# Differential attention scores on one Trainium2 core: six passes on 64 rows in place of four stacked passes on 128 rows

## The chip, the cores and the metric

The kernel runs on 1 core of one Trainium2 chip. The metric is the device time of one execution in microseconds (us). Engines are called as the profile calls them: PE is TensorE's matrix multiply, PEld its weight load, DVE is VectorE, ACT is ScalarE, POOL is GpSimd, SP is SyncE, which issues most DMAs. One measured execution of the kernel before was profiled; its instructions and waits are the trace that is read here.

## The reference, cut to what matters

The program is one step of a decoder layer: RWKV-7 time mixing and differential attention run as two branches on the same normalised input, are merged by gates, and an MLP follows. Float32 throughout. There are 512 prompt tokens and 8 samples of 8 tokens. The change touches the attention over the prompt. Each of the 4 heads has two parts, c = 0 and 1, of 64 channels; each part has its own scores and softmax, and the second softmax is subtracted from the first with a weight:

```python
def diff_attend(q, q_pos, segs, lam, slopes):
    ...
        s = jnp.einsum('bqhcd,bkhcd->bhcqk', q, k).astype(jnp.float32) * scale
        dist = q_pos[:, None] - k_pos[None, :]
        bias = -slopes[:, None, None] * dist.astype(jnp.float32)
        scores.append(jnp.where(dist >= 0, s + bias[None, :, None], NEG))
    p = jax.nn.softmax(jnp.concatenate(scores, axis=-1), axis=-1)
    attn = p[:, :, 0] - lam * p[:, :, 1]
    ...
```

The prompt is attended in blocks of 128 queries, with causal masking, so query block qb needs the first 128(qb+1) keys.

## The kernel before, in words

**Halves.** Products of float32 numbers are made from numbers in a shorter format (`F32R`). Each operand x is split: hi is x copied by ACT to `F32R`, lo is x - hi, made by DVE. A product is then three matmul passes that add up in one bank of PSUM: hi·hi, hi·lo and lo·hi. All dense projections are done so (`stream`, line 154): 8 pieces of 128 input channels, three passes each, 288 columns.

**Stages.** The input is normalised and the projections q, k and v of head 0 are made. Then, for each head h, `qkv(h)` (line 352) makes that head's projections, channels on the 128 rows and tokens along the columns, and `stacks(h)` (line 528) and four calls of `prompt(h, qb)` (line 542) do its attention over the prompt. Part 0 of a head lies in rows 0 to 63 of `qT` and `kT`, part 1 in rows 64 to 127. For heads 0 to 2 this overlaps with the projections of the next head. Beside head 3's blocks run the samples' attention (`sample`, line 622) and the first projections of the RWKV branch. The RWKV branch, the gates, the output projections and the MLP follow.

**The scores before.** `stacks` lays out, for each part cc, three operands of 128 rows by 512 columns. `qs` holds q's hi in the part's own 64 rows and q's lo in the other 64. `ks` holds k's hi in both. `kl` holds k's lo in the part's own rows, and zeros, set once at the start by POOL, in the others. One pass `qs`·`ks` over 128 rows is then hi·hi + lo·hi, and `qs`·`kl` is hi·lo: two passes a part, four a block (lines 548 and 549). For a head that takes six ACT operations and four DVE operations on 64 rows by 512 columns.

**After the scores.** `stt` on DVE scales each part's scores and adds the bias on the way from PSUM to the tile `sc`; DVE takes the maximum, ACT the exponential, DVE joins the two parts, PE transposes the result (`pt`) and multiplies it by v (`po`).

**Banks.** The scores of part cc go into the bank `cbank(cc)` (line 107), of which there is one for each part. The samples' scores use the same two banks, even samples the first and odd ones the second.

**What sets the order.** The kernel is written with priorities. Instructions of attention have the priority of their place in the program; dense passes have a later one (`FILL`), so that they fill in where nothing else is ready, and the evictions and splittings that feed them an earlier one (`FEED`). A scheduler orders each engine's instructions ahead of time, by priority among those that it reckons to be ready, and each engine then works through its list in order. `feed` (line 506) keeps several blocks under way, each at another of its steps, and `fill` (line 224) places a number of dense passes behind what was just issued.

Of the kernel before, what the change touches and what calls it, by code (L numbers as in the profile page):

```python
# [8 lines left out]
F32 = mybir.dt.float32  # L9
F32R = mybir.dt.float32r  # L10
# [5 lines left out]
P = 128  # L16
D = 1024
KT = D // P
NPR = 512
# [22 lines left out]
def tile_hybrid_step(ctx, tc, xT, xsT, ktab, vtab, s0T, ptab, w_in, vecs, w2a2, g2, lamv,  # L42
# [3 lines left out]
    PE, VE, AE, GE = nc.tensor, nc.vector, nc.scalar, nc.gpsimd  # L46
    PS = bass.MemoryType.PSUM

    def pool(name, bufs=1, stack=ctx, **kw):
        return stack.enter_context(tc.tile_pool(name=name, bufs=bufs, **kw))  # L50

    def f32(ap):
        return ap.bitcast(F32)
# [3 lines left out]
    def act(out, in_, func=AF.Copy, **kw):  # L57
        ring["act"] = AE.activation(out=out, in_=in_, func=func, **kw)  # L58

    def tt(out, a, b, op, eng=None):  # L60
        ins = (eng or VE).tensor_tensor(out=out, in0=a, in1=b, op=op)  # L61
        if eng is None:
            ring["tt"] = ins

    def stt(out, a, s, b, op0, op1):
        VE.scalar_tensor_tensor(out=out, in0=a, scalar=s, in1=b, op0=op0, op1=op1)

    def ts(out, a, s1, op0, s2=None, op1=ALU.bypass, eng=None):
        (eng or VE).tensor_scalar(out=out, in0=a, scalar1=s1, scalar2=s2, op0=op0, op1=op1)

    def mm(out, lhsT, rhs, start=True, stop=True):
        ring["mm"] = PE.matmul(out=out, lhsT=lhsT, rhs=rhs, start=start, stop=stop)  # L72
        return ring["mm"]

    def tr(out, in_, idn):
        ring["mm"] = PE.transpose(out=out, in_=in_, identity=idn)
# [14 lines left out]
    MUL, ADD, SUB, MAX = ALU.mult, ALU.add, ALU.subtract, ALU.max  # L91
# [9 lines left out]
    def bank(name):  # L101
        return psw.tile([P, 512], F32, tag="w", name=name)
# [4 lines left out]
    def cbank(i, name):  # L107
        return (psy if i else psc).tile([P, 512], F32, tag=f"c{i}", name=name)
# [131 lines left out]
    def rpow(dst, src, scale, eps):  # L240

        ts(dst, src, scale, MUL, eps, ADD)
        GE.tensor_tensor(out=dst, in0=dst, in1=mhalf[:dst.shape[0], :dst.shape[1]], op=ALU.pow)
# [27 lines left out]
    with tc.tile_pool(name="xin", bufs=2, reuse_waits="tile") as xin:  # L271
# [6 lines left out]
        for k in range(0, KT, 4):  # L278
            for j in range(3):
                with prio(FEED + 1000 + 10 * k + j):  # L280
                    name = f"raw_{'qkv'[j]}0_{k}"
                    if k == 0:
                        raw = ring["pool"].tile([P, 4, P], F32, tag="raw", name=name, bufs=3)
                    else:
                        raw = zw.tile([P, 1 + NX], F32, tag="z" if j else "tz", name=name,
                                      bufs=2 if j else 1)[:, :4 * P].rearrange("p (k w) -> p k w", k=4)
# [46 lines left out]
    ap = pool("ap", stack=attn, reuse_waits="tile")  # L333
    qT = ap.tile([P, HB, NT], F32, name="qT")
    kT = ap.tile([P, HB, NT], F32, name="kT")
# [75 lines left out]
    bp = ap.tile([P, HB, 512], F32, name="bp")  # L411
# [108 lines left out]
        for u in done:  # L520
            flight.remove(u)


    kl = ap.tile([P, 2, NPR], F32R, name="kl")
    for cc in range(2):
        GE.memset(kl[64 - 64 * cc:128 - 64 * cc, cc].bitcast(F32), 0.0)

    def stacks(h):

        qs = ap.tile([P, 2, NPR], F32R, tag="qs", name=f"qs{h}", bufs=1)  # L530
        ks = ap.tile([P, 2, NPR], F32R, tag="ks", name=f"ks{h}", bufs=1)
        for cc in range(2):
            own, oth = slice(64 * cc, 64 * cc + 64), slice(64 - 64 * cc, 128 - 64 * cc)
            q, k = qT[own, h, :NPR], kT[own, h, :NPR]
            act(qs[own, cc], q)
            tt(qs[oth, cc], q, f32(qs[own, cc]), SUB)
            act(ks[own, cc], k)
            act(ks[oth, cc], k)
            tt(kl[own, cc], k, f32(ks[own, cc]), SUB)
        return qs, ks  # L540

    def prompt(h, qb, ot, ss, qs, ks):
        L = P * (qb + 1)
        sc = ap.tile([P, 2, 512], F32, tag="sc", name=f"sc{h}{qb}", bufs=3)
        for cc in range(2):
            pss = cbank(cc, f"pss{h}{qb}{cc}")
            t = slice(qb * P, (qb + 1) * P)
            mm(pss[:, :L], qs[:, cc, t], ks[:, cc, :L], stop=False)
            mm(pss[:, :L], qs[:, cc, t], kl[:, cc, :L], start=False)
            stt(sc[:, cc, :L], pss[:, :L], 0.125, bp[:, h, 512 - L:], MUL, ADD)  # L550
        nmx = stat.tile([P, 2], F32, tag="nmx", name=f"nmx{h}{qb}", bufs=4)
        VE.tensor_reduce(out=nmx, in_=sc[:, :, :L], axis=AX.X, op=MAX, negate=True)
        z = stat.tile([P, 2], F32, tag="z", name=f"z{h}{qb}", bufs=4)
        for cc in range(2):
            act(sc[:, cc, :L], sc[:, cc, :L], AF.Exp, bias=nmx[:, cc:cc + 1],
                accum_out=z[:, cc:cc + 1])
        rz = stat.tile([P, 2], F32, tag="rz", name=f"rz{h}{qb}", bufs=4)
        VE.reciprocal(out=rz, in_=z)
        stt(rz[:, 1:2], rz[:, 1:2], nlam, z[:, 0:1], MUL, MUL)
        stt(sc[:, 0, :L], sc[:, 1, :L], rz[:, 1:2], sc[:, 0, :L], MUL, ADD)  # L560
        yield 1
        pt = bank(f"pt{h}{qb}")
        for kb in range(qb + 1):
            tr(pt[:, kb * P:(kb + 1) * P], sc[:, 0, kb * P:(kb + 1) * P], ident)
        attnT = ap.tile([P, 512], F32, tag="attnT", name=f"attnT{h}{qb}", bufs=3)
        act(attnT[:, :L], pt[:, :L])
        yield 1
        po = bank(f"po{h}{qb}")
        for kb in range(qb + 1):
            mm(po[:, :P], attnT[:, kb * P:(kb + 1) * P], vtok[:, kb, h],  # L570
               start=(kb == 0), stop=(kb == qb))
        ts(ot[:, qb], po[:, :P], rz[:, 0:1], MUL)
        junk = ap.tile([P, P], F32, tag="junk", name=f"junk{h}{qb}", bufs=1)
        act(junk, ot[:, qb], AF.Square, accum_out=ss[:, qb:qb + 1])
        if qb < 3:
            return
        rr = stat.tile([P, 4], F32, tag="rr", name=f"rr{h}")
        rpow(rr, ss, 1.0 / P, 1e-5)
        for qb in range(4):
            ts(ot[:, qb], ot[:, qb], rr[:, qb:qb + 1], MUL)  # L580
        yield 1
        yield 1
        pt = bank(f"pto{h}")
        for qb in range(4):
            tr(pt[:, qb * P:(qb + 1) * P], ot[:, qb], ident)
        obh = ap.tile([P, 512], F32, tag="obh", name=f"obh{h}", bufs=2)
        act(obh, pt, scale=subg)
        nc.gpsimd.dma_start(out=ob_d[h, :, :NPR], in_=obh)
# [76 lines left out]
    for h in range(HB):  # L665
        if h:
            qkv(h)
        for cc in range(2):
            GE.tensor_copy(
                out=qbd[64 * cc:64 * cc + 64, :, h, 8 * cc:8 * cc + 8],  # L670
                in_=qT[64 * cc:64 * cc + 64, h, NPR:].rearrange("p (b q) -> p b q", b=NB))
        ot = ap.tile([P, 4, P], F32, tag="ot", name=f"ot{h}", bufs=2)
        ss = stat.tile([P, 4], F32, tag="ss", name=f"ss{h}")
        qk = stacks(h)
        if h < HB - 1:
            for qb in range(4):
                feed(prompt(h, qb, ot, ss, *qk))
    waiting += [shifted(12), shifted(13)] + zs(0)
    for n in range(4):
        for unit in (prompt(HB - 1, n, ot, ss, *qk), sample(2 * n), sample(2 * n + 1)):  # L680
            feed(unit)
            fill(18)
# [12 lines left out]
    pss = bank("psq")  # L695
# [428 lines left out]
    for i, d in enumerate((0, 4, 1, 5, 2, 6, 3, 7)):  # L1124
# [4 lines left out]
        k = d % 4  # L1129
# [44 lines left out]
    qs = {}  # L1174
# [125 lines left out]
    rows = []  # L1300
    for d, n in enumerate((None, "t1", "b11", "t2", "b21", "t3", "b22", "t4")):
        if n:
            t = fp.tile([P, 2, 4, 288], F32R, tag=f"h_{n}", name=f"w3_{d}", bufs=1)
            t = t.rearrange("p i k t -> p (i k t)")
# [5 lines left out]
    for t0, n in LAST:  # L1310
# [47 lines left out]
        for d in range(KT):  # L1358
# [4 lines left out]
            if d + 1 in ends:  # L1363
                i = ends.index(d + 1)
# [119 lines left out]
```

## Time and profile before

| | |
|---|---|
| median of 3 runs | 1004.05 us (1003.92 to 1005.98) |
| the profiled execution, its own time | 1006.88 us |
| its span, first to last instruction | 1005.1 us |
| mean granted clock of TensorE | 0.993 of full |
| HBM read and written | 89.38 MB and 14.78 MB |
| DMA queue that loads most: share of 16 engines' span | 30.4% |
| score passes (tile `pss`) | 64, first start 39.3 us, last 151.6 us |

In the rows below a time comes first, then how long the instruction took, its engine, the line of the helper that recorded it, the operation, the tile that it writes and the tiles that it reads, the piece of TensorE's array (rows*columns), the shape, and the count. Most matmuls are recorded by one helper on line 72, so they are told apart by their tiles: `pss` is a block's scores, `ps_q`, `ps_k`, `ps_v` and `ps_z` are dense projections, `psb` and `pos` the samples' attention. Matmuls are pipelined: one lasts longer than the time to the start of the next, so what it costs is read from start to start. An idle time in brackets names the instruction that ended it.

### The profile page before, as it was taken

The numbers are of one execution on the slowest core, as the hardware profiler recorded it, in microseconds if no ns is written. First come the engines' busy times: TensorE is split into PE (matmuls) and PEld (weight loads), VectorE is DVE, ScalarE is ACT, GpSimd is POOL, SyncE is SP. The second block draws the span as 40 slices with busy tenths as digits, with TensorE's granted clock in tenths as the row PEclk, the third lists the DMA queues.
The fourth block names the chain that finished last, engine by engine and source line by source line (L and its number), as shares of the span: only waits on it lengthen the run. The fifth ranks groups of instructions, "written<-read, shape, count | busy, mean of one in ns | idle before, by whom it ended". The sixth has DMA issues, their size and how long they took to land.

```text
span 1005.1 us, 24415 instructions
## 1 busy us (share of the span) xinstructions
PE 975.1 (97%) x10012; PEld 919.4 (91%) x10012; DVE 688.9 (69%) x1459; ACT 497.0 (49%) x1094; POOL 87.5 (9%) x171
## 2 busy tenths in 40 slices
PE   9999999899999998999989999999999999999996
PEld 9999998898887887988779999999999999999996
DVE  6698566864946679444579898966666666666644
ACT  6576455354435355453334666644444444444732
POOL 2511001301010340000210000000000000000001
PEclk9999999999989999999999999999999999999999
DMA  7422673211111234323357642222222222221402
GB/s 266 136 70 83 205 223 114 61 64 45 43 59 45 69 106 152 104 81 113 103 182 225 206 140 86 83 95 85 88 92 85 85 84 85 84 87 41 135 3 95
DMA packets 50833, 105.75 MB, mean 105 GB/s; under 512 B 6066, under 2 KB 8114, under 8 KB 50594
## 3 DMA queue, kind: packets, MB, share of 16 engines
q1 hardware_dynamic: 47442, 96.95, 30.4%
q0 software_dynamic: 1648, 5.35, 1.5%
q8 instruction: 79, 1.29, 0.5%
q10 hardware_dynamic: 1632, 1.89, 0.5%
q14 instruction: 32, 0.26, 0.1%
HBM read 89.38 MB, written 14.78 MB: 104 GB/s over the span
## 4 chain that ended last, share of the span: by engine, by line
PE 83%; DVE 6%; ACT 4%; issue 3%; DMA 2%; POOL 1%; SPq 0%; DVEq 0%; ACTq 0%; POOLq 0%
PE ps_dn L72 20%; PE ps_g L72 8%; PE ps_z L72 8%; PE ua L1220 5%; PE ux L1220 5%; PE ps_wo L72 4%; PE ps_k L72 3%; PE uc L1220 3%; PE ub L1220 3%; PE ud L1220 2%; PE ps_bra L72 2%; PE ps_q L72 2%; PE pch L72 2%; PE ps_brb L72 2%; PE ps_v L72 2%
## 5 line engine op out<-in xcount | busy, mean ns | idle before, releaser
L72 PE MATMUL ps_dn<-q,hi_dn 128*128 128x288 f32 x768 | 154.7, 296 | 0.0
L72 PEld LDWEIGHTS ps_dn<-q,hi_dn 128*128 128x128 f32 x768 | 122.7, 188 | 1.4
L72 PE MATMUL ps_dn<-q,lo_dn 128*128 128x288 f32 x384 | 113.2, 295 | 0.0
L72 PE MATMUL ps_g<-xl,hi_g 128*128 128x288 f32 x256 | 79.7, 311 | 0.0
L72 PE MATMUL ps_g<-xh,hi_g 128*128 128x288 f32 x256 | 79.0, 309 | 0.0
L72 PE MATMUL ps_g<-xh,lo_g 128*128 128x288 f32 x256 | 79.0, 309 | 0.0
L72 PEld LDWEIGHTS ps_dn<-q,lo_dn 128*128 128x128 f32 x384 | 72.0, 188 | 0.0
L72 PE MATMUL ps_z<-xh,lo_z 128*128 128x288 f32 (+1 forms) x224 | 68.9, 308 | 0.0
L72 PE MATMUL ps_z<-xh,hi_z 128*128 128x288 f32 (+1 forms) x224 | 67.6, 302 | 0.0
L72 PE MATMUL ps_z<-xl,hi_z 128*128 128x288 f32 (+1 forms) x224 | 66.8, 298 | 0.0
L61 DVE TENSOR_TENSOR ya<-ya,ps_dn 128x288 f32<-128x288 f32 x96 | 43.2, 451 | 29.4 <-PE ps_dn L72 29.4
L58 ACT ACTIVATE hi_dn<-raw_dn 128x512 fp32r<-128x512 f32 x48 | 30.1, 628 | 57.0 <-PE ps_dn L72 57.0
L1220 PE MATMUL ua<-h_b,hi 128*128 128x288 f32 x256 | 53.2, 298 | 0.0
L1220 PE MATMUL ux<-h_t,hi 128*128 128x288 f32 x256 | 52.3, 296 | 0.0
L58 ACT ACTIVATE c<-c 128x288 f32<-128x288 f32 x112 | 48.4, 439 | 7.4 <-DVE c L61 5.8
L72 PEld LDWEIGHTS ps_g<-xh,hi_g 128*128 128x128 f32 x256 | 48.7, 190 | 3.1 <-issue 1.8
L72 PEld LDWEIGHTS ps_g<-xl,hi_g 128*128 128x128 f32 x256 | 48.6, 190 | 1.9
L72 PEld LDWEIGHTS ps_g<-xh,lo_g 128*128 128x128 f32 x256 | 48.6, 190 | 1.6 <-DVE lo_g L61 0.2
L58 ACT ACTIVATE hi<-a 128x1024 fp32r<-128x1024 f32 (+1 forms) x32 | 27.1, 846 | 42.0 <-PE ps_dn L72 34.2
L72 PE MATMUL ps_dn<-q,w 128*128 128x320 f32 (+1 forms) x336 | 46.3, 297 | 0.0
L61 DVE TENSOR_TENSOR lo<-s,hi 128x1024 fp32r<-128x1024 f32 x32 | 39.2, 1224 | 10.1 <-ACT hi L58 10.0
L72 PEld LDWEIGHTS ps_dn<-q,w 128*128 128x128 f32 x336 | 45.3, 190 | 0.1
(395 smaller groups left out, 2802.2 us busy)
## 6 DMA issues: line engine op xcount, KB each, us to landing
a<-in_w_up_dram SPq DMA_DIRECT2D x32, 512.0 KB, 3.4
raw_dn<-in_w_down_dram SPq DMA_DIRECT2D x64, 256.0 KB, 2.8
raw_g<-in_w_in_dram SPq DMA_DIRECT2D x32, 256.0 KB, 3.1
raw_z<-in_w_in_dram SPq DMA_DIRECT2D x28, 256.0 KB, 3.1
gt_d<-gg SPq DMA_DIRECT2D x16, 288.0 KB, 2.4
g<-gt_d SPq DMA_DIRECT2D x16, 288.0 KB, 3.6
kp<-in_ktab_dram SPq DMA_DIRECT2D x16, 256.0 KB, 4.5
vp<-in_vtab_dram SPq DMA_DIRECT2D x16, 256.0 KB, 3.8
```

The lines of the kernel that those rows point to most:

```text
L58: ring["act"] = AE.activation(out=out, in_=in_, func=func, **kw)
L61: ins = (eng or VE).tensor_tensor(out=out, in0=a, in1=b, op=op)
L72: ring["mm"] = PE.matmul(out=out, lhsT=lhsT, rhs=rhs, start=start, stop=stop)
L1220: ring["mm"] = PE.matmul(out=ps[:, :288], lhsT=l[:, k], rhs=hb[blk][:, h, k], start=start and i == 0, stop=i == 11, skip_group_check=skip)
```

## The change

`stacks` no longer lays out stacked copies. It makes the hi and the lo of q and of k once, each a tile of all 128 rows by 512 columns, part 0 in the upper and part 1 in the lower 64 rows: two ACT and two DVE operations a head. `prompt` takes both banks at once and issues three passes a part, hi·hi, hi·lo and lo·hi, each on the part's own 64 rows of the array, part 0 and part 1 in turn. The two scaled copies out of PSUM stand behind all six passes. The tile `kl` and its two memsets on POOL are gone. The same three products are added up as before.

```diff
-    kl = ap.tile([P, 2, NPR], F32R, name="kl")
-    for cc in range(2):
-        GE.memset(kl[64 - 64 * cc:128 - 64 * cc, cc].bitcast(F32), 0.0)
...
-        qs = ap.tile([P, 2, NPR], F32R, tag="qs", name=f"qs{h}", bufs=1)
-        ks = ap.tile([P, 2, NPR], F32R, tag="ks", name=f"ks{h}", bufs=1)
-        for cc in range(2):
-            own, oth = slice(64 * cc, 64 * cc + 64), slice(64 - 64 * cc, 128 - 64 * cc)
-            q, k = qT[own, h, :NPR], kT[own, h, :NPR]
-            act(qs[own, cc], q)
-            tt(qs[oth, cc], q, f32(qs[own, cc]), SUB)
-            act(ks[own, cc], k)
-            act(ks[oth, cc], k)
-            tt(kl[own, cc], k, f32(ks[own, cc]), SUB)
-        return qs, ks
+        out = []
+        for n, t in (("q", qT), ("k", kT)):
+            hi, lo = (ap.tile([P, NPR], F32R, tag=f"{n}{x}", name=f"{n}{x}{h}", bufs=1) for x in "hl")
+            act(hi, t[:, h, :NPR])
+            tt(lo, t[:, h, :NPR], f32(hi), SUB)
+            out.append((hi, lo))
+        return out
...
+        two = [cbank(cc, f"pss{h}{qb}{cc}") for cc in range(2)]
+        t = slice(qb * P, (qb + 1) * P)
+        for i, (q, k) in enumerate(((qs[0], ks[0]), (qs[0], ks[1]), (qs[1], ks[0]))):
+            for cc in range(2):
+                rows = slice(64 * cc, 64 * cc + 64)
+                mm(two[cc][:, :L], q[rows, t], k[rows, :L], start=(i == 0), stop=(i == 2))
         for cc in range(2):
-            pss = cbank(cc, f"pss{h}{qb}{cc}")
-            t = slice(qb * P, (qb + 1) * P)
-            mm(pss[:, :L], qs[:, cc, t], ks[:, cc, :L], stop=False)
-            mm(pss[:, :L], qs[:, cc, t], kl[:, cc, :L], start=False)
-            stt(sc[:, cc, :L], pss[:, :L], 0.125, bp[:, h, 512 - L:], MUL, ADD)
+            stt(sc[:, cc, :L], two[cc][:, :L], 0.125, bp[:, h, 512 - L:], MUL, ADD)
```

## The prediction, made before the result was known

> **What bounds the kernel now.** I read the page's totals first, then the chain of work that ended last, then the busy time of the attention stage by windows, and last TensorE's timeline there.
>
> ```profile
> span 1005.1 us, 24415 instructions
> ...
> PE 975.1 (97%) x10012; PEld 919.4 (91%) x10012; DVE 688.9 (69%) x1459; ACT 497.0 (49%) x1094; POOL 87.5 (9%) x171
> ...
> PE 83%; DVE 6%; ACT 4%; issue 3%; DMA 2%; POOL 1%; SPq 0%; DVEq 0%; ACTq 0%; POOLq 0%
> ```
>
> TensorE (PE) is busy for 97% of the span and holds 83% of the chain. The score passes lie in the stage from 35 to 155 us. The windows view gives, for two of its 20 us stretches, the busy time of PE, weight load, DVE, ACT and POOL, then the granted clock (1.00):
>
> ```profile
> 35.00:55.00 20.00, 19.86 (x140) 18.33 (x138) 18.54 (x43) 15.07 (x39) 11.56 (x36) 1.00 0.33 101
> 55.00:75.00 20.00, 19.62 (x144) 18.68 (x145) 19.14 (x49) 13.77 (x42) 3.29 (x5) 1.00 0.25 81
> ```
>
> The stage is PE-bound with VectorE (DVE) close behind: 19.14 of 20 us. Between score passes PE runs the dense projections of the next head, which need none of this head's scores. So a microsecond more or less of PE's own time moves all that follows by the same amount, while latency inside a score block is mostly covered by dense work.
>
> **What a pass costs.** Matmul durations overlap, so I take start to start. From TensorE's timeline, two neighbouring passes of each width 128, 256, 384 and 512, all in head 3, where the four passes of a block stand together:
>
> ```profile
> 111.96 0.27 PE L72 MATMUL pss<-ks,qs 128*128 128x128 f32 x1
> 112.07 0.27 PE L72 MATMUL pss<-kl,qs 128*128 128x128 f32 x1
> ...
> 124.02 0.28 PE L72 MATMUL pss<-ks,qs 128*128 128x256 f32 x1
> 124.14 0.28 PE L72 MATMUL pss<-kl,qs 128*128 128x256 f32 x1
> 124.35 0.64 PE L72 MATMUL pos<-vp,pT 128*32 128x128 f32 x16
> 124.81 0.40 PE L72 MATMUL pos<-vtok,pT 128*32 128x128 f32 x8
> 125.14 0.33 PE L76 MATMUL pts<-cst_sb,scs 128*128 128x128 f32 x1
> ...
> 137.37 0.34 PE L72 MATMUL pss<-ks,qs 128*128 128x384 f32 x1
> 137.54 0.33 PE L72 MATMUL pss<-kl,qs 128*128 128x384 f32 x1
> ...
> 151.37 0.39 PE L72 MATMUL pss<-ks,qs 128*128 128x512 f32 x1
> 151.60 0.40 PE L72 MATMUL pss<-kl,qs 128*128 128x512 f32 x1
> ```
>
> P, the price of one pass, is 0.11, 0.12, 0.17 and 0.23 us for the four query blocks: 0.63 us a head, 2.52 us over four heads. The kernel makes four passes a block, the change six, in three pairs on rows 0 to 63 and 64 to 127. If a pair takes the time of one pass, each block saves one P: **-2.52 us** over all.
>
> The same rows price a change of the array's shape. From the last 128*128 pass to the first 128*32 matmul there are 0.21 us instead of 0.12: 0.09 to enter. The sixteen matmuls from 124.35 take 0.46 us, 0.029 each; the eight from 124.81 would take 0.23 at that rate and take 0.33: 0.10 to leave. The new passes have the shape 64*128, all around them is 128*128, so each of the 16 blocks pays 0.19: 3.04 us. Three blocks of head 3 leave into a 128*32 group as now (124.14 is followed by one), where a switch is paid already: 0.3 less, so **+2.74 us**.
>
> Do two 64-row tiles run side by side? The trace has no pair that shares its output columns, as the new ones do. The nearest rows are pairs of 64*64 tiles that share neither rows nor columns:
>
> ```profile
> 304.80 0.45 PE L72 MATMUL pY<-SVU,ABR 64*64 64x64 f32 x8
> 305.17 0.41 PE L72 MATMUL ps_g<-xh,hi_g 128*128 128x288 f32 x1
> ```
>
> Eight take 0.37 us, 0.27 without the 0.10 to leave: 0.034 each. [...] Bounds for a new pair: P (fully side by side) and 2P (in turn). I take P, to which the 64*64 rows are nearer. [...]
>
> **Whether the pairs stay together.** This decides the sign. Instructions are issued in order of priority among those that are ready, and part 0 and part 1 write two banks. Each bank opens when the scaled copy of the block before has left it, and the two copies run one after the other on DVE. Its group, and a block that is torn now (head 0, last query block, TensorE's timeline):
>
> ```profile
> L66 DVE SCALAR_TENSOR_TENSOR sc<-pss,bp x32: 280/478/693, 41.6 to 152.3; 128x128 f32<-128x128 f32 x8, 128x256 f32<-128x256 f32 x8, 128x384 f32<-128x384 f32 x8, 128x512 f32<-128x512 f32 x8
> ```
>
> ```profile
> 45.43 0.40 PE L72 MATMUL pss<-ks,qs 128*128 128x512 f32 x1
> ...
> 47.76 0.40 PE L72 MATMUL pss<-ks,qs 128*128 128x512 f32 x1
> ```
>
> Part 1 starts 2.3 us after part 0, with dense work between. Going through the timeline, 10 of the 12 blocks of heads 0 to 2 have other work inside, 2 have not; head 3's four are whole. Three of the ten are the first blocks of heads, torn because the halves of q and k come one by one; the change makes one half serve both parts, so their pairs hold, but the three pairs may come apart: one more switch each way, 3 x 0.19 = 0.57 us (bounds 0 and 1.14). The other seven (256 wide twice, 384 twice, 512 three times) have P summing to 0.24 + 0.34 + 0.69 = 1.27. One copy lasts 0.28 to 0.69 us, about two or three passes, so part 0 runs its passes 1 and 2 alone, its third beside part 1's first, and part 1 ends alone: 5P instead of 3P, +2P each: **+2.54 us**. Bounds: 0 if the pairs hold, and 6P with a second switch, 3P + 0.19 each: 3.81 + 1.33 = 5.14. I take the middle, because the copy's length lies between one pass and three.
>
> The added wait is the same thing seen from the queue: part 1's first pass now stands second in its block. Behind it, if issued early, are part 0's other passes and the dense matmuls; part 0's copy on DVE waits for them. Its price is at most one copy, 0.69 us a block, 4.8 us for the seven, inside the bound 5.14.
>
> **What ACT and DVE lose.** The preparation, from its tiles' views, then the same operations on 128 rows:
>
> ```profile
> L58 ACT ACTIVATE qs<-qT x8: 617/631/636, 36.3 to 99.0; 64x512 fp32r<-64x512 f32 x8
> L61 DVE TENSOR_TENSOR qs<-qT,qs x8: 684/686/729, 38.1 to 99.9; 64x512 fp32r<-64x512 f32 x8
> ```
>
> ```profile
> L58 ACT ACTIVATE ks<-kT x16: 611/630/636, 36.8 to 106.7; 64x512 fp32r<-64x512 f32 x16
> L61 DVE TENSOR_TENSOR kl<-kT,ks x8: 677/690/735, 38.8 to 106.7; 64x512 fp32r<-64x512 f32 x8
> ```
>
> ```profile
> L58 ACT ACTIVATE hi_z<-raw_z 128x512 fp32r<-128x512 f32 x11 | 6.9, 628 | 7.7 <-PE ps_z L72 2.1 <-issue 1.9 <-ACT osT L58 1.7
> L61 DVE TENSOR_TENSOR lo_z<-raw_z,hi_z 128x512 fp32r<-128x512 f32 x10 | 6.9, 690 | 4.2 <-ACT hi_z L58 3.7 <-PE ps_z L72 0.2
> ```
>
> 64 rows cost what 128 cost. ACT goes from 24 operations of 0.63 us to 8 (-10.1 us), DVE from 16 of 0.69 to 8 (-5.5 us). Little of it is on the path; PE's waits between 35 and 160 us (waits view, what PE waited for, us, times, longest) bound it:
>
> ```profile
> PE pv L76 <- DVE vT L61: 0.6, 1, 0.6
> PE pt L76 <- DVE scs L66: 0.5, 1, 0.5
> PE pss L72 <- DVE qs L61: 0.4, 1, 0.4
> PE pss L72 <- ACT ks L58: 0.3, 1, 0.3
> ```
>
> ```profile
> 54.59 0.29 PE L72 MATMUL ps_v<-xh,lo_v 128*128 128x288 f32 x1
> 55.24 0.30 PE L72 MATMUL pss<-ks,qs 128*128 128x128 f32 x1 [0.37 <-DVE qs L61]
> ```
>
> The gap is 0.65 us where a dense pass takes 0.13, so a lost 0.52 shows as 0.37: add 0.15 to each wait. The two waits for q and k halves are worth 1.0 us, all four 2.4 us. Bounds: 0 and -2.4. I take the two that this preparation causes, **-1.0 us**; late next are those two passes' own banks. The removed memsets on POOL have nobody waiting. The copy of part 0 now starts after the fifth pass rather than the second; DVE's queue and then the exponentials stand behind it, and dense work on PE covers them. If that cover failed at a block it would cost two passes, at most 0.46 us. DMAs and queues are not moved.
>
> **Sum:** -2.52 + 2.74 + 2.54 + 0.57 - 1.0 = **+2.3 us**. The profiled execution took 1006.88 us in all for a span of 1005.1, so it would become about 1009.2; against the median of 1004.05 the forecast is **1006.4 us**. I count 0.2%, 2.0 us, as what a measurement can tell apart.
>
> **Rivals.**
>
> *The relief decides (faster).* Only if the banks open within one pass of each other, so that all pairs hold, and DVE, freed of 5.5 us, is on time at all four waits. Then -2.52 + 2.74 - 2.4 = -2.2: 1001.9 us. For it: DVE's 19.14 of 20 us. Against it: the ten torn blocks. It turns where DVE's lead exceeds the longest wait, 0.6 + 0.15 us. [...]
>
> *No side by side.* Tiles that share output columns run in turn: six passes, +2 x 2.52 instead of -2.52, so 5.04 + 2.74 + 0.57 - 1.0 = +7.3: 1011.4 us, as order no longer matters. The change would not do what it says. For it: no row shows such a pair. Against it: the 64*64 pairs.
>
> **How the numbers follow.** Forecast case 0.46, its own range from 1004.5 (half of the 2.54, no extra switch) to 1009.6 (5.14 and 1.14 for the torn blocks): of it 0.32 is slower by over 0.2%, 0.14 within. Pairs hold with a small relief, 0.20, within. Relief decides, 0.20, faster. No side by side, 0.14, slower. Faster 0.20, same 0.34, slower 0.46. The range 1001.5 to 1009.6 leaves out the lower part of the faster rival (0.07) and most of the last rival (0.12).
>
> **What would show it.** In the profile after: passes of shape 64*128 whose two parts start within some 0.01 us of each other where they stand paired, and one P apart from pair to pair; a first dense pass 0.09 to 0.10 us late on either side of each block; in heads 0 to 2 blocks where part 0 runs two passes before part 1's first; eight ACT and eight DVE operations of 0.63 and 0.69 us for the halves; the two waits of PE for q and k halves gone. I am wrong if the blocks come out whole in most of the 12, if paired starts are a full P apart, or if PE's busy time in the stage falls while the time does not.

## The result, and the profile after

The changed kernel takes 1010.64 us (median of 6, 1010.42 to 1011.68) against 1004.73 us (1003.6 to 1006.54) for the kernel before: the ratio is 1.0055 [1.0042, 1.0068], by which it is 5.5 us slower (the medians differ by 5.9). The forecast was slower too, by 2.3 us; the measured time lies 1.0 us above the upper end of the range.

The page of the kernel after, its totals and its chain of work (the profiled execution took 1010.68 us, at a mean granted clock of 0.992):

```profile
span 1008.9 us, 24453 instructions
...
PE 981.6 (97%) x10044; PEld 919.8 (91%) x10044; DVE 684.0 (68%) x1451; ACT 486.8 (48%) x1078; POOL 86.5 (9%) x169
...
PE 86%; DVE 5%; ACT 3%; issue 2%; POOL 2%; DMA 1%; SPq 0%; DVEq 0%; ACTq 0%; POOLq 0%
```

DVE and ACT have less to do, as foreseen (4.9 and 10.2 us), and the time has risen all the same. PE's share of the chain has gone from 83% to 86%. The windows view of the kernel after, in the two stretches shown of before:

```profile
35.00:55.00 20.00, 20.00 (x128) 16.65 (x127) 17.37 (x41) 10.60 (x30) 10.82 (x36) 1.00 0.31 101
55.00:75.00 20.00, 20.00 (x140) 16.89 (x139) 16.54 (x43) 11.38 (x39) 1.63 (x3) 1.00 0.16 48
```

PE is now "busy" for all of both stretches, and gets through 128 and 140 instructions instead of 140 and 144, at a full clock. So each instruction holds PE for longer, and the busy share doesn't show it. It has to be read from start to start. TensorE's timeline of the kernel after, around a whole block of 512 keys in head 3; "x2" is a pair that started together:

```profile
156.19 0.29 PE L72 MATMUL ps_z<-xl,hi_z 128*128 128x288 f32 x1
156.41 0.50 PE L72 MATMUL pss<-kh,qh 64*128 64x512 f32 x2
156.75 0.40 PE L72 MATMUL pss<-kl,qh 64*128 64x512 f32 x2
156.99 0.39 PE L72 MATMUL pss<-kh,ql 64*128 64x512 f32 x2
157.31 0.53 PE L72 MATMUL pos<-vp,pT 128*32 128x128 f32 x12
```

The middle pair takes 0.24 us, where one 512-wide pass took 0.23 before: the two parts do run side by side. But the first pair takes 0.34, the last 0.32, and the dense pass ahead of the block 0.22, not its usual 0.13. A block in head 0 (the same view, part 1 of the last query block) shows the fourth edge, and a tear:

```profile
46.25 0.29 PE L72 MATMUL ps_k<-xh,hi_k 128*128 128x288 f32 x1
46.38 0.29 PE L72 MATMUL ps_k<-xl,hi_k 128*128 128x288 f32 x1
46.60 0.49 PE L72 MATMUL pss<-kh,qh 64*128 64x512 f32 x1
46.94 0.39 PE L72 MATMUL pss<-kl,qh 64*128 64x512 f32 x1
47.17 0.39 PE L72 MATMUL pss<-kh,ql 64*128 64x512 f32 x1
47.49 0.40 PE L72 MATMUL ps_k<-xh,lo_k 128*128 128x288 f32 x1
47.73 0.29 PE L72 MATMUL ps_k<-xh,hi_k 128*128 128x288 f32 x1
```

Part 0's three passes ran alone at 44.74 us, 1.86 us earlier; here part 1's run alone. When part 0 started, the copy out of part 1's bank (the second 384-column copy of the block before) had not begun; whole timeline:

```profile
44.74 0.50 PE L72 MATMUL pss<-kh,qh 64*128 64x512 f32 x1
44.80 0.55 DVE L66 SCALAR_TENSOR_TENSOR sc<-pss,bp 128x384 f32<-128x384 f32 x1
```

And what a **visit**, a run of 64*128 passes among 128*128 ones, costs beside its passes can be read off at four places: 0.09 on the dense pass before it (0.22 for 0.13), 0.11 on its first pass (0.34 for 0.23), 0.09 on its last (0.32 for 0.23), and 0.11 on the first dense pass behind it (0.24 for 0.13). That is **0.40 us a visit**. Where the passes are 128 columns wide it is 0.35, as the first pass is then only some 0.05 above P (from 40.19 to 40.35 us, 0.16 for 0.11). The timeline has 27 visits: 4 in head 3, and 23 for the 12 blocks of heads 0 to 2. Four of these 12 are whole, three are torn into part 0's three passes and part 1's three, and five are in other pieces.

Where the time arises: the last dense `ps_v` pass, which ends heads 0 to 2, comes 5.43 us later than before; the last score pass 5.39; the last matmul of tile `pq`, behind the stage, 5.73 (at 175.79 instead of 170.06 us). Nearly all of it arises in heads 0 to 2; head 3, with four whole blocks, adds 0.3 us.

The preparation and PE's waits, from the groups by line and the waits view (35 to 165 us) of the kernel after:

```profile
L58 ACT ACTIVATE qh<-qT x4: 617/625/633, 36.4 to 104.1; 128x512 fp32r<-128x512 f32 x4
L61 DVE TENSOR_TENSOR ql<-qT,qh x4: 677/702/723, 38.1 to 104.9; 128x512 fp32r<-128x512 f32 x4
L58 ACT ACTIVATE kh<-kT x4: 619/627/634, 36.9 to 110.1; 128x512 fp32r<-128x512 f32 x4
L61 DVE TENSOR_TENSOR kl<-kT,kh x4: 683/686/700, 38.7 to 110.8; 128x512 fp32r<-128x512 f32 x4
```

```profile
PE pt L76 <- DVE sc L66: 0.7, 2, 0.5
PE pv L76 <- DVE vT L61: 0.6, 1, 0.6
```

Eight ACT and eight DVE operations, as forecast, and the two waits for halves of q and k are gone. The transposes `pt` wait for `sc` 0.7 us in all; before they waited as long, 0.2 us for `sc` and 0.5 for `scs`.

### The profile page after: what moved, and what is told of

It reads as the page before. It is cut to its first block, busy times and chain, and to the rows that moved or that the text cites. A ratio compares the mean times of both kernels' runs of the same rounds, so it can differ in the third digit from the quotient of the medians.

```text
span 1008.9 us, 24453 instructions
## 1 busy us (share of the span) xinstructions
PE 981.6 (97%) x10044; PEld 919.8 (91%) x10044; DVE 684.0 (68%) x1451; ACT 486.8 (48%) x1078; POOL 86.5 (9%) x169
## 4 chain that ended last, share of the span: by engine, by line
PE 86%; DVE 5%; ACT 3%; issue 2%; POOL 2%; DMA 1%; SPq 0%; DVEq 0%; ACTq 0%; POOLq 0%
PE ps_dn L72 20%; PE ps_g L72 9%; PE ps_z L72 8%; PE ua L1214 5%; PE ux L1214 5%; PE ps_wo L72 4%; PE ps_k L72 3%; PE ps_v L72 3%; PE uc L1214 3%; PE ps_q L72 3%; PE ub L1214 3%; PE ud L1214 2%; PE ps_bra L72 2%; PE pch L72 2%; PE pA L72 2%
## 5 line engine op out<-in xcount | busy, mean ns | idle before, releaser
L61 DVE TENSOR_TENSOR lo<-s,hi 128x1024 fp32r<-128x1024 f32 x32 | 39.2, 1224 | 10.1 <-ACT hi L58 10.0
```

## The experiments

The theory (V) was that the visits cost the time: the new shape is entered and left more often, and at a higher price, than I had reckoned. The first rival (O) was the order of the work: both banks taken together, the copies behind all passes, so that PE waits. The second was that the relief of ACT and DVE, not seen as a gain, was real and only covered by something larger. Ratios are against the kernel before, run on the same chip; "the stage" is the start of the last `pq` matmul less before's 170.06 us. It is good to about 1 us, since the last matmul of tile `pst`, ahead of all scores, itself starts between 27.3 and 28.6 us in these traces (28.3 before).

**Six passes without the new shape.** The kernel after, with q's halves laid out a part at a time and padded with zeros to 128 rows: the same six passes a block, the same order and banks, all 128*128, so none beside another. The products added are the same.

```diff
+    qz = [ap.tile([P, 2, NPR], F32R, name=f"q{x}") for x in "hl"]
+    for x in qz:
+        for cc in range(2):
+            GE.memset(x[64 - 64 * cc:128 - 64 * cc, cc].bitcast(F32), 0.0)
...
-                rows = slice(64 * cc, 64 * cc + 64)
-                mm(two[cc][:, :L], q[rows, t], k[rows, :L], start=(i == 0), stop=(i == 2))
+                mm(two[cc][:, :L], q[:, cc, t], k[:, :L], start=(i == 0), stop=(i == 2))
```

> The changed kernel with its order kept (both banks taken at once, both copies behind all six passes), but no 64-row shape: q's halves lie in tiles whose other 64 rows are zero, so all six passes are 128*128. Theory V (visits): the changed kernel loses by its 27 visits to the 64*128 shape, 0.40 us each (10.8 us); without them, but with 24 pass slots a head instead of about 15 (15.1 us instead of 9.6), it comes out about 5 us faster than the changed kernel: 1005.3, at most 1007. Rival O (order): the later copies and the joint banks hold up DVE and with it PE; then it stays at the changed kernel's 1010.6 or, with 5.5 us more of passes, goes to 1016.

Measured: 1009.41 us, 1.0048 [1.0034, 1.0063], +4.8 us; the stage +5.2. TensorE's timeline of this kernel, the block shown above:

```profile
155.41 0.30 PE L72 MATMUL ps_z<-xl,hi_z 128*128 128x288 f32 x1
155.54 0.62 PE L72 MATMUL pss<-kh,qh 128*128 128x512 f32 x2
156.00 0.63 PE L72 MATMUL pss<-kl,qh 128*128 128x512 f32 x2
156.47 0.63 PE L72 MATMUL pss<-kh,ql 128*128 128x512 f32 x2
157.03 0.43 PE L72 MATMUL pos<-vp,pT 128*32 128x128 f32 x8
```

"x2" here is two passes in turn: 0.46 and 0.47 us, 0.23 each, with 0.13 for the dense pass before them. There is no edge, but for the 0.09 of the last two (0.56 us from 156.47 to 157.03), ahead of a 128*32 group; the kernel before has 0.10 at the same place (151.60 to 151.93 us, 0.33 for 0.23). The kernel has two passes a block more than before, 2 x 2.52 = 5.04 us, and is 4.8 to 5.2 us slower. So the passes explain all of it; the order, which it shares with the kernel after, and its preparation (three ACT and three DVE operations a head) add and take nothing that shows. The expectation by V, 1005.3, was too low because it took the 27 visits at their full 10.8 us, and rival O's, 1010.6 or more, was a little too high. The kernel after has 5.5 us less of passes than this one (9.6 instead of 15.1) and is no faster: about that much is what the 64-row shape costs it in all. Six passes side by side with their visits cost as much as six whole ones without.

**Before's passes in the new order.** The kernel before with both banks taken together, its four passes alternating and the copies behind them.

```diff
+        two = [cbank(cc, f"pss{h}{qb}{cc}") for cc in range(2)]
+        t = slice(qb * P, (qb + 1) * P)
+        for i, k in enumerate((ks, kl)):
+            for cc in range(2):
+                mm(two[cc][:, :L], qs[:, cc, t], k[:, cc, :L], start=(i == 0), stop=(i == 1))
```

> The kernel before with the changed order alone: both banks are taken at once, part 0 and part 1 alternate (four 128*128 passes), and both copies stand behind the last pass. Theory V (visits): no visit to the 64-row shape, so no loss: 1004, within 1 us of the kernel before. Rival O (order), by what the held kernel still lost: the copies come later, DVE is late for the transposes, 2 to 3 us slower, 1006.5.

Measured: 1005.66 us, 1.001 [0.9999, 1.002]; the stage +0.1 us. The order alone costs at most 2 us, and in the stage nothing. For the four whole passes rival O falls; the held blocks below have an order of their own, with waits of its own.

**The old preparation back.** The kernel after, with four ACT and two DVE operations a head on 64 rows added, into a tile that nobody reads: as many operations as before.

```diff
+        spare = ap.tile([P, 2, NPR], F32R, tag="spare", name=f"spare{h}", bufs=1)
+        for cc in range(2):
+            own = slice(64 * cc, 64 * cc + 64)
+            act(spare[own, 0], qT[own, h, :NPR])
+            act(spare[own, 0], kT[own, h, :NPR])
+            tt(spare[own, 1], kT[own, h, :NPR], f32(out[1][0][own]), SUB)
```

> The changed kernel with the kernel before's load on ACT and DVE put back: four ACT and two DVE operations more a head, on 64 rows by 512 columns, into a tile that nothing reads. If the lighter preparation is worth the 1.0 us of the prediction: 1 us slower than the changed kernel, 1011.6 (up to 2.4 us, 1013). If ACT and DVE were never what PE waited for: 1010.6, or a little less, since two visits fewer come out of its order.

Measured: 1010.62 us, 1.0064 [1.0051, 1.0076]. The stage is +5.4 us, the kernel after's own +5.7. The ratios, 1.0064 and 1.0055, differ by less than their intervals: 10.1 us of ACT (16 operations of 0.63) and 5.5 us of DVE (8 of 0.69) given back cost 0.9 us at the likeliest by the ratios, and nothing in the stage. But PE does wait more. Its waits view, 35 to 176 us, has three groups that the kernel after has not:

```profile
PE pss L72 <- DVE sc L66: 0.8, 2, 0.5
PE po L72 <- ACT attnT L58: 0.3, 1, 0.3
PE pss L72 <- DVE nlam L69: 0.3, 1, 0.3
```

That is 1.4 us of waits more, and this kernel's order has 25 visits instead of 27, which takes up to 0.8 us off. So the relief is small, and these runs don't show whether it is nothing or the forecast's 1.0 us.

**The price of a visit by itself.** Two kernels from the one before, each with one more pass of 128 keys behind each block, into a bank that nobody reads. They differ only in the rows of that pass, 128 or 64:

```diff
+        with tc.issue_after(ring["mm"].ins), prio(FEED):
+            mm(tbank(f"dummy{h}{qb}")[:, :P], qs[0:64, 0, t], ks[0:64, 0, :P])
```

> The kernel before with one more pass behind the last score pass of each block: 128 rows, 128 columns, into a bank that nothing reads. 16 passes of 0.11 us and a little for the place: +1.8 us against the kernel before, 1006.5, by all theories. It is the partner of the next run.

> As the run before, at the same 16 places, but the extra pass uses only rows 0 to 63, so that each is one visit to the 64*128 shape with one pass in it. Theory V, by the one-pass visits in the changed kernel's timeline (0.35 us beyond the pass): 16 x 0.35 = 5.6 us more than with 128 rows, 1012. By the prediction's price of 0.19: 3.0 us more, 1009.5. If the shape is free and only the torn order costs: the same as with 128 rows, 1006.5.

Measured: 1007.16 us, 1.0028 [1.0017, 1.0038], with 128 rows; 1009.39 us, 1.0048 [1.0034, 1.0061], with 64. TensorE's timelines of the two at the same place, first with 128 rows:

```profile
82.46 0.33 PE L72 MATMUL pss<-ks,qs 128*128 128x384 f32 x1
82.63 0.33 PE L72 MATMUL pss<-kl,qs 128*128 128x384 f32 x1
82.80 0.22 PE L72 MATMUL dummy<-ks,qs 128*128 128x128 f32 x1
82.86 0.34 PE L72 MATMUL ps_v<-xl,hi_v 128*128 128x288 f32 x1
83.04 0.30 PE L72 MATMUL ps_v<-xh,lo_v 128*128 128x288 f32 x1
```

and with 64:

```profile
83.23 0.34 PE L72 MATMUL pss<-ks,qs 128*128 128x384 f32 x1
83.40 0.33 PE L72 MATMUL pss<-kl,qs 128*128 128x384 f32 x1
83.67 0.32 PE L72 MATMUL dummy<-ks,qs 64*128 64x128 f32 x1
83.92 0.40 PE L72 MATMUL ps_v<-xl,hi_v 128*128 128x288 f32 x1
```

From the start of the pass before it to the start of the pass behind it: 82.63 to 82.86, 0.23 us, and 83.40 to 83.92, 0.52 us; the dense pass behind then takes 0.18 and 0.24. A visit of one pass costs 0.35 us here. Place by place, from the last score pass to the end of the pass behind the extra one, the kernel with 64 rows takes 0.28 to 0.35 us longer among dense passes, 0.19 to 0.29 where other work follows, and 0.1 or nothing at three places where PE waited in the kernel with 128 rows: 3.9 us over the 16 blocks, where 16 times 0.35 would be 5.6. The two medians differ by 2.2 us, the stages by 1.7 (+1.4 and +3.2), or by 2.9 counted from `pst`, which starts at 28.5 and 27.4 us in these two traces. So the timelines show the price of a visit, and about half of the 5.6 us, or less, reaches the end. The time by itself, 1009.39 us, is just what the forecast's 0.19 would give (1009.5); it doesn't tell the two prices apart.

**Blocks held whole.** The kernel after, with part 1 first (its bank opens last) and the other five passes placed right behind it with the earlier priority: 16 visits instead of 27, all of six passes. The order of the parts and the products within the sum are other ones.

```diff
+        def part(cc, i):
+            q, k = ((qs[0], ks[1]), (qs[0], ks[0]), (qs[1], ks[0]))[i]
+            rows = slice(64 * cc, 64 * cc + 64)
+            mm(two[cc][:, :L], q[rows, t], k[rows, :L], start=(i == 0), stop=(i == 2))
+        part(1, 0)
+        with tc.issue_after(ring["mm"].ins), prio(FEED):
+            for cc, i in ((0, 0), (1, 1), (0, 1), (1, 2), (0, 2)):
+                part(cc, i)
```

> The changed kernel with the six passes of a block held together: part 1, whose bank opens last, goes first, q's hi times k's lo stands ahead because it is ready last, and the other five passes follow at once at high priority. 16 visits instead of 27, all pairs side by side. Theory V: 11 visits of 0.40 us and 2.0 us of unpaired passes fall away, -6.4 us against the changed kernel: 1004.2, about the kernel before. Rival O: the order of copies is as late as in the changed kernel or later, so 1010 or more. Rival P (pairs are no gain as such): no more than the 4.4 us of the visits, 1006.2.

Measured: 1006.58 us, 1.003 [1.0016, 1.0044]; the stage +2.2 us. Nearly half of the loss is gone. Theory V's 1004.2 was too low by 2.4 us; rival P's 1006.2 is nearer. A part of what is left shows in the waits view of this kernel, 35 to 176 us:

```profile
PE pt L76 <- DVE sc L66: 1.9, 4, 0.6
PE pv L76 <- DVE vT L61: 0.6, 1, 0.6
```

With the six passes together, the transposes `pt` of the block come to the head of PE's list before DVE has made the joined `sc`: four waits, 1.9 us, up from two of 0.7. PE's waits of all kinds add up to 2.8 us here and to 2.3 in the kernel before, so they are not all that is left.

**The transposes later.** One more step (`yield 1`) between the softmax and the transposes, so that more dense passes lie ahead of them: in the held kernel, in the kernel before as its control, and in the changed kernel as it is.

```diff
         yield 1
+        yield 1
         pt = bank(f"pt{h}{qb}")
```

> The held kernel with the transposes of a block's weights one step later in the order, so that DVE has one more step to finish them. The held kernel's timeline lost 1.9 us, some 2.5 us with the hidden part, in four waits of PE's transposes for DVE. If that is all that 16 whole visits still cost: 1004.2, the kernel before. If the visits themselves keep costing more than the pairs give back: it stays at 1006 to 1007.

> The kernel before with the same later transposes, as the control. Its timeline has 0.7 us in two such waits: 1003.3 to 1004.2. If it gains as much as the held kernel does, the later step is a gain of its own and says nothing on the visits.

> The changed kernel, nothing held, with the transposes one step later. Its order then has 21 visits, with two blocks of head 0 torn in the middle, where the changed kernel has 27. Theory V, counted from the held and late kernel (16 visits, 0.15% below the kernel before): 5 more visits of 0.40 us, and 3P more in the two torn blocks of 384 and 512 columns (0.51 + 0.69 us): 3.2 us more, 1.7 us above the kernel before. If the changed kernel's loss was nothing but the waits of the transposes: as the held and late kernel, 1.5 us below the kernel before. If neither matters: it stays 5.5 us above.

Measured: held and late 1004.47 us, 0.9985 [0.9972, 0.9997]; before and late 1004.49 us, 0.9992 [0.9977, 1.0007]; after and late 1006.76 us, 1.0018 [1.0004, 1.0033]. The stage: -1.1, -2.3 and +1.0 us (-0.2, -1.9 and +1.9 counted from `pst`). The waits view of the held and late kernel, 35 to 176 us:

```profile
PE pss L72 <- DVE sc L66: 0.7, 2, 0.4
PE pv L76 <- DVE vT L61: 0.6, 1, 0.6
PE pbs L76 <- POOL rss L243: 0.4, 1, 0.4
PE po L72 <- ACT attnT L58: 0.2, 1, 0.2
```

The wait of `pt` is gone, and the held kernel gains 4.5 us (1.0030 to 0.9985), 3.3 in the stage. The control gains from the same line too, 0.8 us by its ratio and 2.3 in the stage, so the step is in part a gain of its own, and what the wait cost the held kernel beyond that lies between 1.0 us (by the stage) and 3.7 (by the ratios). The changed kernel gains 3.7 us, partly for another reason: its blocks come in 21 visits instead of 27. Held and late is the one version that is faster than the kernel before, by 1.5 us [0.3, 2.8]; but the control with the stacked passes comes to the same median, and the two can't be told apart. The side-by-side passes themselves are worth nothing that shows here.

**The parts in turn.** The held kernel with part 1's three passes first and then part 0's, meant to undo the side-by-side running alone.

```diff
-            for cc, i in ((0, 0), (1, 1), (0, 1), (1, 2), (0, 2)):
+            for cc, i in ((1, 1), (1, 2), (0, 0), (0, 1), (0, 2)):
```

> The held kernel (six passes of a block together, 16 visits), with part 1's three passes first and part 0's three behind them, so that only one of the six stands beside a pass of the other part: 5P a block instead of 3P, and 19 visits. If a pair really takes the time of one pass: 2 x 2.52 = 5.0 us for the passes and 1.2 us for the visits more than the held kernel's 1006.6: 1012.8. If pairs gain nothing: the visits alone, 1007.8.

Measured: 1016.49 us, 1.0118 [1.0102, 1.0134]. It did not do what it was meant to. TensorE's timeline of this kernel, head 3:

```profile
163.13 0.51 PE L72 MATMUL pss<-kl,qh 64*128 64x512 f32 x2
163.47 0.41 PE L72 MATMUL pss<-kh,qh 64*128 64x512 f32 x2
163.71 0.40 PE L72 MATMUL pss<-kh,ql 64*128 64x512 f32 x2
164.04 0.43 PE L72 MATMUL pos<-vp,pT 128*32 128x128 f32 x8
```

Part 0's passes stand behind all of part 1's in the program, and still start with them. PE's list, too, has part 1's three passes and then part 0's three for this block. So side by side holds without alternation. The loss has another source, which the windows view of this kernel shows; the granted clock is the third number from the end:

```profile
44.00:48.00 4.00, 4.00 (x12) 2.32 (x10) 1.88 (x5) 1.62 (x6) 0.47 (x1) 0.50 0.36 147
...
88.00:92.00 4.00, 4.00 (x14) 2.95 (x13) 1.02 (x5) 1.09 (x4) 0.00 (x0) 0.50 0.00 0
```

The held kernel in the first of these stretches:

```profile
44.00:48.00 4.00, 4.00 (x28) 3.43 (x27) 3.77 (x11) 3.27 (x10) 0.58 (x2) 1.00 0.59 213
```

TensorE ran at half clock for 6.8 us twice in the stage, and got through 12 instructions instead of 28. That loses about 6.8 us of the 9.9 between the two kernels; where the rest arises is open. So this kernel doesn't price the passes in turn.

**Every block torn.** The held kernel in turn, with a 128-row pass of 128 keys, into a bank that nobody reads, between the parts: meant to be 32 visits of three unpaired passes. The trace has 30, as halves of neighbouring blocks meet twice.

```diff
+            part(1, 1)
+            part(1, 2)
+            mm(tbank(f"dummy{h}{qb}")[:, :P], qs[0][:, t], ks[0][:, :P])
+            for i in range(3):
+                part(0, i)
```

> The held kernel with every block torn on purpose: part 1's three passes, one extra 128-row pass of 128 columns into a bank that nothing reads, then part 0's three passes. 32 half-blocks instead of 16 whole blocks, no pass beside another. Theory V: 16 more visits of 0.35 to 0.40 us (5.6 to 6.4), 3P a block more (7.6 us), 16 extra passes (1.8 us): 15 us more than the held kernel's 1006.6, 1021 to 1022. If tearing costs visits only, since the parts would not run side by side anyway: 1014 to 1015. More than 1022 if the granted clock falls, as it did in the run with the parts in turn.

Measured: 1026.42 us, 1.0198 [1.0176, 1.0219], by the ratios 19.9 us over before and 16.9 over the held kernel. Here too the clock fell. The windows view of this kernel:

```profile
48.00:52.00 4.00, 4.00 (x14) 2.87 (x13) 1.08 (x2) 1.54 (x5) 0.00 (x0) 0.50 0.00 0
```

The clock was at half from about 42 to 55.5 us, and for another 3.4 us between 64 and 72 us. Dense passes took 0.24 us there instead of 0.13 (TensorE's timeline, 66.03 to 68.91 us). Half of these 17 us, some 8.5, is lost to that by my estimate from the clock. What is left, some 8.4 us, is little more than half of V's 15, and no more than the 7.4 to 8.4 us of the expectation by which tearing costs visits only. So this kernel doesn't bear out V's price of a tear.

**A failed one.** To take two waits for halves from the kernel before, its second copy of k's hi went from ACT to POOL.

```diff
-            act(ks[oth, cc], k)
+            GE.tensor_copy(out=ks[oth, cc], in_=k)
```

> The kernel before with two of the six ACT operations of a head's preparation (k's hi into the other part's 64 rows) moved to POOL: ACT has 5.0 us less in the stage. If PE's waits for q's and k's halves are worth 1.0 us there, up to 1 us faster than the kernel before: 1003. If they only move on, or POOL's slower copy is late itself: 1004 to 1006.

Measured: 1014.0 us, 1.0091 [1.0076, 1.0106]. Its waits view:

```profile
PE pss L72 <- POOL ks L538: 7.8, 3, 6.6
```

The copies queued behind POOL's other work, and PE stood for 6.6 us at once. The windows view shows that the clock fell while PE stood (0.71 on the mean from 40 to 44 us, where PE ran nothing) and was at half until 52 us:

```profile
40.00:44.00 4.00, 0.00 (x0) 0.00 (x0) 1.55 (x3) 0.40 (x2) 3.70 (x18) 0.71 0.02 8
44.00:48.00 4.00, 1.65 (x7) 1.65 (x8) 0.00 (x0) 0.00 (x0) 3.76 (x9) 0.50 0.21 83
48.00:52.00 4.00, 4.00 (x19) 4.00 (x19) 2.21 (x8) 0.00 (x0) 0.01 (x1) 0.51 0.18 74
```

It says nothing about relief, only that POOL was the wrong place.

## Why the prediction was right and wrong

**Right: the direction, and much of the mechanism.** Pairs run side by side at one P (0.24 us for 512 columns, where one pass of before took 0.23), so "no side by side" falls. No row of the kernel before shows what such a pair costs; P for it was an estimate, and the runs bear it out. Blocks do come apart because part 1's bank opens one copy later: in the three that are torn into two halves, part 0 started at 42.51, 44.74 and 58.55 us, and the copy that opens part 1's bank ended at 43.00, 45.34 and 59.41 us. Head 1's last block (65.85 and 66.93 us) comes apart though both banks were open at 65.03 us, which isn't explained. The switches outweigh the saving. The preparation takes the operations and durations forecast.

**Wrong: the price of a switch.** This is the step that failed: "0.09 to enter" and "0.10 to leave", 0.19 us a block. It counts one interval at each end, taken from a 128*32 group, and none of the visit's own first and last pass. The 64*128 rows show two intervals at each end: 0.09 + 0.11 to enter, 0.09 + 0.11 to leave, 0.40 together. The forecast's term for switches, +3.3 us, came to some 6.7, as the sum below shows; at 0.19 the 27 visits would make 4.8 of it.

**Wrong: the number of visits.** The forecast had 19 (16 and three more for the first blocks); its upper bounds together come to 29 (seven and three more), and there are 27. "This decides the sign" was wrong too: with all 16 blocks whole the held kernel is still 3.0 us slower than before, and only the later transposes bring it level.

**Right in size, in part by luck: the passes that run alone.** "+2.54" measures 2.0 us (slots of 9.6 us in the timeline, where 7.56 would be all paired). But no block ran two passes of part 0 ahead of a pair, as forecast. Three of the seven blocks that were to be torn came whole; two, and one that was not among the seven, came as 3 + 3 passes, at 3P more instead of 2P.

**Not settled: the relief.** "-1.0" for two waits. These waits did go. The ratio and the stage of the kernel with the old preparation show no loss beyond their noise, while its waits grow by 1.4 us; in the kernel with padded passes other waits came in their place (2.3 us in all, 2.0 before). So it lies between nothing and some 1.4 us.

The sum again, from starts of matmuls between 39 us and the last `pq`. Passes by their P: 10.08 us before, 9.5 after (the first pair, at 37.6 us, lies ahead of it): -0.6. All above P in the score passes and their dense neighbours, edges and stalls together: 4.4 before (2.0 in the passes, 2.4 in the neighbours), 8.9 after (5.3 and 3.6): +4.5. The attention's other matmuls (the transposes, `po`, `pv` and `pos`): 26.1 before, 27.7 after: +1.7. All else: +0.1. Together +5.7, as from the first of these starts to the last.

Two of these lines hold more of the switch than they show. The 4.4 of before has the two waits for halves in it, some 1.0 us by the forecast's count, which are gone after; without them the edges and stalls grew by 5.5. And of the +1.7, 1.2 lies on twelve matmuls that stand right beside a visit: they take 2.4 us, the twelve beside score passes before 1.2. So the switch, "+2.74" and "+0.57" in the forecast, 3.3 us, comes to some 6.7 us; the passes, 0.0 in the forecast, to -0.6; and the two waits, by this count, to the -1.0 forecast. Some 0.6 us is left that this doesn't place.

Twenty-seven visits at 0.35 to 0.40 would be over 10 us. Why only some 6.7 is lost isn't shown. Some edges meet a wait or another shape: three of head 3's visits leave into a 128*32 group, where the kernel before pays as well (0.09 at 124.14 us, 0.10 at 151.60).

What the tears alone cost is shown only together with the waits: the held kernel takes 2.5 us off (1.0055 to 1.0030), after 11 visits fewer would have taken 11 x 0.40 + 2.0 = 6.4, and the waits of `pt` that came, 1.9 us instead of 0.7, gave part of it back.

**Open:** why only about half of the dummy visits' price, or less, reached the end; why the kernel with every block torn lost less than the visits' price says; what makes the clock fall; and whether held and late is faster than before and late, or slower, by less than 2 us.

## What to carry to other kernels

Price a change of the array's shape by all that it slows, the last pass before, the first and the last in it and the first behind (0.09, 0.11, 0.09 and 0.11 us here), and multiply by the visits that the scheduler will make of a block, not by the blocks. Four passes on the whole array beat six on halves here, though these do run side by side, because the saving, 2.5 us, is six visits' worth. ACT's and DVE's work, given back to the kernel after, showed in PE's waits (1.4 us more) and not in the stage (+5.4 us beside +5.7); put the work that a change takes off an engine back as a dummy, and read both, before counting on it.

## What the runs showed of the hardware

- A run of 64*128 passes among 128*128 ones costs 0.40 us beside its passes, 0.35 if they are 128 columns wide (156.19 to 157.31 us in the kernel after; 83.40 us in the kernel with an extra 64-row pass). Not all of it reaches the end of the stage: of 16 one-pass visits, 5.6 us at 0.35, the stage shows 1.7, or 2.9 counted from `pst`.
- The two halves of the rows work through their passes each on its own: three passes of part 1 followed in the program by three of part 0 ran in three pairs (163.13 to 163.71 us), so alternation wasn't needed there. With a 128*128 pass between the parts, in the kernel with every block torn, the two parts of a block ran one after the other (39.33 to 39.60 and 40.06 to 40.34 us, the extra pass at 39.80).
- In the two kernels with the parts in turn the granted clock was 0.50 for 6.8 us twice, and for about 13.5 us from 42 us on, in stretches where the profile has PE busy for 4.00 of 4.00 us. With every block torn, visits stood ahead of that stretch (39.33 to 41.60 us) and of the 3.4 us at half clock from 65.7 us on (60.34 to 65.03 us); but through visits from 91.29 to 95.32 us the clock was 1.00, and the dense passes behind them took 0.13 us. And it was 0.50 too in the kernel with the copies on POOL, from within the 6.6 us in which PE stood until 52 us, so the shape is not the only thing that goes before it. What sets it off wasn't tried.
